# A hybrid decoder trunk on one core: the planner that spreads side work over the mixer's steps prices VectorE and TensorE operations anew

## The chip, the core and the metric

The kernel runs on one core of one Trainium2 chip, in one launch. The metric is device microseconds (us) of one execution; the time of a kernel is the median of several runs. A core has TensorE (PE in the rows; PEld is its weight loads), VectorE (DVE), ScalarE (ACT), GpSimd (POOL) and SyncE (SP), each with a queue of its own that it works through in order, and 16 DMA engines that all queues share.

## The reference, cut to what matters

One residual layer over 1024 tokens of width 1024. A mixer projects the normalised input once and runs three branches on it (stick-breaking attention, native sparse attention, a gated linear recurrence), gates and merges them and adds the result to the residual. Then a PEER layer chooses, for each token and each of 8 heads, 16 experts of 16384, and adds their output:

```python
h = rms_norm(x, norm_mix[l])
x = x + hybrid_mixer(h, ...)
h = rms_norm(x, norm_ffn[l])
x = x + peer_ffn(h, peer_w_q[l], peer_sub_keys[l], peer_u[l], peer_v[l])
...
s = jnp.einsum("nhad,akd->nhak", qh, sub_keys)
top_s, top_i = lax.top_k(s, K)
...
hpre = jnp.einsum("nd,nhkd->nhk", xc, u_tab[eidx])
act = gate * jax.nn.gelu(hpre)
return jnp.einsum("nhk,nhkd->nd", act, v_tab[eidx])
```

## The kernel before

The tokens are cut into four parts of 256 (parts 0 to 3). The mixer goes through the parts in order and through four heads or head groups in each. Its main work stands in a list of items, three to a head: the recurrence (`hg_items`), sparse attention (`nsa_items`) and stick-breaking attention (`sb_items`). An item has up to four stages, and the main loop (`while t < N + 3 or todo`) gives out, at step t, one stage each of items t, t-1, t-3 and t-2. There are 456 items. This text calls a head's stretch a round: round 2.3 is part 2, head 3, and begins where the recurrence's decay scan of that head (`b_hg`, L782) stands on VectorE.

All other work of the mixer is side work, cut into pieces (class `Piece`), each with an earliest and a latest step: the projections that feed a round (`pj_...`, each 24 matmuls of 256 columns at L265), the gates, and a part's tail: eight merges of the branches (`merge`, `pb` and `sg`), eight output projections (`wo`, `pj_wo`, with the residual's adds at L941), norms, the scores of the PEER router (`score_pieces`, `ts`) and the routing itself (`route`, tiles ending in `_rt`). For the middle parts 1 and 2, whose experts are computed densely, the routing is also spread into a matrix (`spread_pieces`): 64 blocks for each of these parts, 128 in all. A block is two operations on VectorE (L1219 and L1220, tile `hot`, 128x1024 in f16), eight small matmuls (L1223 and L1224, `gb`) and a copy on ScalarE; every fourth block writes 1 MB of the matrix `d_G` to memory.

Where a piece goes is decided by an estimate. `account()` adds to `load_["DVE"]` and `load_["PE"]` a price for each instruction given out. After each step the loop raises what is due: by `RDVE` (3.0) on VectorE, and on TensorE by 3.5, or by `PD` (1.2) times what VectorE got in this step where that is more, at most twice 3.5. As long as the load of an engine is below what is due, the next ready piece is given out: pieces marked `vector` (routing and spreading) on VectorE's account, all others on TensorE's:

```python
dv = load_["DVE"] - last_dve[0]
rate = min(max(rate, PD * dv), 2 * rate)
due[e] = min(max(due[e] + rate, load_[e] - 3 * rate), load_[e] + 2 * rate)
...
while load_[e] < due[e]:
    p = next((p for p in todo if ... p.ready(t + 1)), None)
```

A piece whose latest step comes is given out whatever the loads say. After the last item the loop goes on until no spread block is left; with each second of these blocks it gives out one piece of the tail of part 3 (list `ending`). What is left of `ending` goes, three pieces to an expert block, into the dense stage.

The dense stage follows: 128 expert blocks, each with 24 matmuls of 512 columns for the hidden values (`g`, L265), the factor from `d_G` (`gt`, L1434) and 24 matmuls for the output (`acc` and `g` at L1441). Parts 0 and 3 take their experts from memory by index: 1024 gathers of 128 rows (512 KB each), issued by GpSimd (L1149, L1159) and used by VectorE (L1151 `u`, L1161 `gacc`). Of these, 420 are tied to steps of the mixer (`paced()`: in proportion to `p + PB`, p being TensorE's estimated load of the step); the rest run beside the dense stage, and those of part 3 (512) need the routing of part 3.

In the end a scheduler of the language's library sets the order on each engine, from the order in which the program gives the work out.

## Time and profile before

| | |
|---|---|
| median of 3 runs | 3502.45 us (3502.05 to 3503.18) |
| the profiled execution | 3511.97 us, of which its span 3510.2 us |
| busy TensorE, VectorE, ScalarE, GpSimd | 3199.7, 3000.6, 1556.4, 1361.7 us |
| mean granted TensorE clock | 0.942 |
| bytes moved by DMA | 1058 MB, 301 GB/s over the span |

The profile's windows give, for a stretch of the span, each engine's busy time, the clock that TensorE was granted (1 is full speed) and the mean busy share of the 16 DMA engines. The chain of waits goes back from the end of a stretch to what released each step. The groups by line give busy time, mean ns of one instruction, and the idle time before them with what ended it. VectorE's busy time counts overlapping starts once, so it lies a little below the sum of its instructions' durations.

### The profile page before, as it was taken

The page shows a single profiled execution, that of the slowest core. Times are in us where ns is not written, and L with a number is a line of the kernel's source. Part 1 is how long each engine was busy: PE and PEld are TensorE (multiplying, and loading weights), DVE is VectorE, ACT ScalarE, POOL GpSimd, SP SyncE. Part 2 cuts the span into 40 slices and gives each one's busy share as a digit, 9 for nine tenths or more (in the row PEclk, how much of TensorE's full clock was granted, in tenths as well). Part 3 has the DMA queues.
Part 4 walks back from the last instruction along what each step waited for, and adds up shares of the span by engine and source line. Part 5 has one row for each costly group of instructions (what it writes and reads, how often), then busy time and mean ns, then how long its engine had stood idle before and what let it go on. Part 6 is the DMA issues. An engine that isn't in the chain of part 4 may idle for free.

```text
span 3510.2 us, 56907 instructions
## 1 busy us (share of the span) xinstructions
PE 3199.7 (91%) x20564; PEld 2175.3 (62%) x20564; DVE 3000.6 (85%) x6666; ACT 1556.4 (44%) x3181; POOL 1361.7 (39%) x1170
## 2 busy tenths in 40 slices
...
GB/s 305 334 248 147 308 185 226 320 314 310 358 284 231 199 289 291 327 332 259 191 250 154 344 372 312 241 271 387 392 384 329 385 367 362 362 368 375 367 358 219
DMA packets 359283, 1058.00 MB, mean 301 GB/s; under 512 B 35236, under 2 KB 107573, under 8 KB 354391
## 3 DMA queue, kind: packets, MB, share of 16 engines
...
q8 instruction: 161, 2.64, 0.3%
...
## 4 chain that ended last, share of the span: by engine, by line
PE 49%; DVE 23%; DMA 11%; issue 8%; ACT 6%; POOL 2%; SPq 0%; DVEq 0%; POOLq 0%; ACTq 0%
PE g L265 13%; PE acc L1441 10%; PE pj_mg L265 4%; DVE u L1151 3%; DVE gacc L1161 3%; PE g L1441 3%; DMA u<-in_peer_u_dram,gidx 3%; PE pj_r_hg L265 2%; DMA v<-in_peer_v_dram,gidx 1%; PE pb L265 1%; DMA gt<-d_G 1%; PE pj_wo L265 1%; POOL v L1159 1%; PE z_sb L417 1%; DMA vraw<-in_peer_v_dram 1%
## 5 line engine op out<-in xcount | busy, mean ns | idle before, releaser
L1159 POOL DMA_INDIRECT v<-in_peer_v_dram,gidx x421 | 556.0, 1321 | 674.0 <-DVE gacc L1161 348.4
L1149 POOL DMA_INDIRECT u<-in_peer_u_dram,gidx x417 | 529.7, 1270 | 596.6 <-DVE u L1151 367.4
L265 PE MATMUL g<-h,us 128*128 128x512 f16 x3072 | 688.2, 381 | 14.8 <-ACT ge L1400 12.1
L1441 PE MATMUL acc<-vs,ac 128*128 128x512 f16 x2304 | 542.2, 383 | 39.9 <-ACT vs L220 23.5
L1441 PEld LDWEIGHTS <-ac 128*128 128x128 f16 x3072 | 303.1, 99 | 426.1 <-issue 66.8
L1161 DVE SCALAR_TENSOR_TENSOR gacc<-v,act,gacc 128x1024 f32<-128x1024 f32 x421 | 538.9, 1280 | 29.4 <-DMA v<-in_peer_v_dram,gidx 25.8
L265 PEld LDWEIGHTS <-us 128*128 128x128 f16 x3072 | 301.6, 98 | 383.0 <-issue 21.1
L1151 DVE SCALAR_TENSOR_TENSOR u<-u,gh 128x1024 f32<-128x1024 f32 x417 | 501.9, 1219 | 33.2 <-DMA u<-in_peer_u_dram,gidx 32.7
L1400 ACT ACTIVATE ge<-g 128x512 f32<-128x512 f32 x128 | 76.1, 596 | 520.7 <-PE g L265 500.1
L265 PE MATMUL pj_mg<-hT,w_mg 128*128 128x256 f16 x2304 | 273.8, 275 | 4.0 <-ACT mg L885 4.0
L265 PEld LDWEIGHTS <-w_mg 128*128 128x128 f16 x2304 | 228.2, 100 | 33.6 <-issue 6.6
L1441 PE MATMUL g<-vs,ac 128*128 128x512 f16 x768 | 190.5, 388 | 11.6 <-ACT ge L1400 11.6
L1149 POOL DMA_INDIRECT rr_u<-in_peer_u_dram,gidx x95 | 134.2, 1413 | 96.7 <-DVE rr_u L1151 49.8
L221 DVE SCALAR_TENSOR_TENSOR vs<-vraw,vs 128x1024 f16<-128x1024 f32 x128 | 154.1, 1219 | 18.6 <-ACT vs L220 18.5
L221 DVE SCALAR_TENSOR_TENSOR us<-uraw,us 128x1024 f16<-128x1024 f32 x128 | 156.1, 1219 | 10.4 <-ACT us L220 10.3
L265 PE MATMUL pb<-o,w_b 128*128 128x256 f16 x1152 | 144.7, 281 | 21.1 <-DVE sg L923 15.1
L1159 POOL DMA_INDIRECT rr_v<-in_peer_v_dram,gidx x90 | 123.0, 1367 | 102.2 <-DVE gacc L1161 81.4
L220 ACT ACTIVATE vs<-vraw 128x1024 f16<-128x1024 f32 x128 | 131.0, 1046 | 55.0 <-DMA vraw<-in_peer_v_dram 55.0
L220 ACT ACTIVATE ac<-ge 128x512 f16<-128x512 f32 x128 | 79.9, 628 | 168.3 <-DVE ge L1434 139.0
L1434 DVE TENSOR_TENSOR ge<-ge,gt 128x256 f32<-128x256 f32 x256 | 98.4, 422 | 58.7 <-ACT ge L1400 44.9
L1223 PE MATMUL gb<-hot 128*128 128x128 f16 x512 | 125.7, 294 | 24.3 <-ACT stage L1226 13.1
L220 ACT ACTIVATE us<-uraw 128x1024 f16<-128x1024 f32 x128 | 134.2, 1048 | 21.4 <-PE g L265 12.8
...
## 6 DMA issues: line engine op xcount, KB each, us to landing
uraw<-in_peer_uT_dram SPq DMA_DIRECT2D x128, 512.0 KB, 7.7
vraw<-in_peer_v_dram SPq DMA_DIRECT2D x128, 512.0 KB, 7.2
...
gt<-d_G SPq DMA_DIRECT2D x32, 1024.0 KB, 17.5
...
```

Of the source, the lines that this page charges most:

```text
L220: S.activation(hi, src, AF.Copy, scale=scale)
L221: V.scalar_tensor_tensor(lo, in0=src, scalar=scale, in1=hi, op0=ALU.mult, op1=ALU.subtract)
L265: P.matmul(ps, l[:, k, :], r[:, k, :], start=(i == 0), stop=(i == n - 1))
L417: P.matmul(x["z"], qz[:, hh, tl * 128:(tl + 1) * 128], st["k"][:, r0 + c0:r0 + c1], start=True, stop=(c0 > 0))
L1149: G.indirect_dma_start(out=ur, out_offset=None, in_=a["peer_u"], in_offset=bass.IndirectOffsetOnAxis(ap=idx[:, c:c + 1], axis=0))
L1151: V.scalar_tensor_tensor(ur, in0=ur, scalar=1.0, in1=h2, op0=ALU.mult, op1=ALU.mult, accum_out=hpre[:, c:c + 1])
L1159: G.indirect_dma_start(out=vr, out_offset=None, in_=a["peer_v"], in_offset=bass.IndirectOffsetOnAxis(ap=idx[:, c:c + 1], axis=0))
L1161: V.scalar_tensor_tensor(acc, in0=vr, scalar=act[:, c:c + 1], in1=acc, op0=ALU.mult, op1=ALU.add)
L1223: P.matmul(ps[:, n, :], hs[:, 0, :, n], hs[:, 2, :, n], start=True, stop=False)
L1400: S.activation(ge, ps, AF.Gelu, scale=1.0 / (SW * SH2))
L1434: V.tensor_tensor(gv, gv, gt[:, :, i % 8, :], op=ALU.mult)
L1441: P.matmul(ps, ac[:, x, t * 128:(t + 1) * 128], v[:, y, dh * 512:(dh + 1) * 512], start=start and n == 0, stop=stop and n == 2)
```

## The change

Three prices and two rates are changed. An operation on VectorE cost 0.06 + n/960 us in the estimate, with n the elements of a partition; it costs 0.15 + n/960 now, with n halved where all operands have 16 bits, doubled for a scan, and 0.08 more for a search or replacement of maxima. A matmul on TensorE cost its columns at 2.4 GHz, four times that in 32 bits; it costs at least 0.11 now, and a transpose 0.11. `RDVE` goes from 3.0 to 3.45 and `PD` from 1.2 to 1.04. No operation is added, removed or altered.

```diff
--- before.py
+++ after.py
@@ -21,7 +21,7 @@
 
 
 
-RPE, RDVE, REND, PD = 3.5, 3.0, 5.0, 1.2
+RPE, RDVE, REND, PD = 3.5, 3.45, 5.0, 1.04
 
 PACE0, PACE, PB = 135, 420, 3.0
 
@@ -1099,10 +1099,16 @@
 
         ins = nc.cur_bb.bb.instructions
         for i in ins[seen[0]:]:
+            aps = [o for o in [*i.outs, *i.ins] if len(getattr(o, "ap", ())) > 1]
             if i.engine == mybir.EngineType.DVE:
-                load_["DVE"] += 0.06 + max([math.prod([x[1] for x in o.ap[1:]]) for o in [*i.outs, *i.ins] if len(getattr(o, "ap", ())) > 1] or [0]) / 960.0
+                n = max([math.prod([x[1] for x in o.ap[1:]]) for o in aps] or [0])
+                half = aps and all(mybir.dt.size(o.dtype) == 2 for o in aps)
+                twice = getattr(i, "is_tensor_tensor_scan", False)
+                more = 0.08 if isinstance(i, (mybir.InstMaxIndex, mybir.InstMatchReplace)) else 0.0
+                load_["DVE"] += 0.15 + more + n / 960.0 * (0.5 if half else 2.0 if twice else 1.0)
             elif i.engine == mybir.EngineType.PE:
-                load_["PE"] += math.prod([x[1] for x in i.outs[0].ap[1:]]) / 2400.0 * (4 if i.ins[0].dtype == F32 else 1)
+                n = math.prod([x[1] for x in i.outs[0].ap[1:]]) / 2400.0
+                load_["PE"] += 0.11 if i.is_transpose else max(0.11, n * (4 if i.ins[0].dtype == F32 else 1))
         seen[0] = len(ins)
 
     total_ = [0.0, 0.0]
```

What the new prices move can be read from the order of the two built programs. Up to round 2.0 (the first two parts) hardly anything moves. From there on, these counts differ (spread blocks, route operations and gathers by their place on VectorE, matmuls by their place on TensorE; "after items" begins with the first merge of part 3 and ends with the first dense block):

| round | spread blocks | route operations | gathers | `pj_wo` matmuls | `gb` matmuls |
|---|---|---|---|---|---|
| 2.0 | 0, 0 | 0, 0 | 44, 44 | 106, 168 | 0, 0 |
| 2.1 | 0, 0 | 1, 41 | 43, 45 | 86, 24 | 0, 0 |
| 2.2 | 1, 8.5 | 175, 135 | 32, 36 | 0, 0 | 0, 40 |
| 2.3 | 30, 47.5 | 0, 0 | 45, 42 | 0, 0 | 216, 376 |
| 3.0 | 16, 8 | 0, 0 | 34, 38 | 132, 48 | 144, 96 |
| 3.1 | 16, 0 | 1, 0 | 46, 42 | 60, 144 | 144, 0 |
| 3.2 | 5, 2 | 175, 170 | 34, 35 | 0, 0 | 8, 0 |
| 3.3 | 30, 46 | 0, 6 | 30, 30 | 0, 0 | 240, 352 |
| after items | 30, 16 | 0, 0 | 32, 31 | 120, 24 | 272, 160 |
| dense stage | 0, 0 | | | 72, 168 | 0, 0 |

In each pair the first number is of the kernel before, the second of the changed one. Other matmuls that move: in 2.2, 82 more of `pj_r_hg` and 24 more of `pj_i_hg`; in 2.3, 157 projection matmuls fewer (72 of them `pj_r_hg`); in 3.0, 61 projection matmuls more; in 3.2, 96 more of `pj_mg`, which 3.3 loses. The loop after the last item takes 22 steps where it took 36, and 60 pieces of `ending` are left for the dense stage where 53 were.

Three places on VectorE show it. The first is the start of round 2.3; `hot8` is the block of dense tokens 8 to 11, so the blocks stand in the order 0, 4, 8 and so on. Before:

```order
L1219 TENSOR_TENSOR hot0_14390<-iorep_139,spread1_14081 128x1024
L776 COPY_PREDICATED lf_hg3_2_14225<-tiny_hg3_2_14223,lf2_hg3_2_14228 128x256
L221 SCALAR_TENSOR_TENSOR hT3_14086<-tr_n3_0_0_14106,hT3_14086 128x4x128
L1220 TENSOR_TENSOR hot0_14390<-hot0_14390,spread1_14081 128x1024
L782 SCALAR_TENSOR_TENSOR b_hg3_2_14233<-lf_hg3_2_14225 128x128 x2
L791 TENSOR_TENSOR att_hg3_2_14305<-pd_hg3_2_14306,packed_106 128x256
L221 SCALAR_TENSOR_TENSOR hT3_14086<-tr_n3_0_1_14113,hT3_14086 128x4x128
L237 TENSOR_TENSOR u_n3_1_14131<-y_n3_1_14128 128x1
L238 TENSOR_TENSOR u_n3_1_14131<-u_n3_1_14131,ms_n3_1_14126 128x1
L239 TENSOR_SCALAR u_n3_1_14131<-u_n3_1_14131 128x1
L240 TENSOR_TENSOR y_n3_1_14128<-y_n3_1_14128,u_n3_1_14131 128x1
L291 SCALAR_TENSOR_TENSOR ht_n3_1_14122<-x_3_1_14120,y_n3_1_14128,gm3_14087 128x1024
```

And in the changed kernel (L1225 and L1226 are the same two lines, moved by six):

```order
L1225 TENSOR_TENSOR hot28_14519<-iorep_139,spread1_13990 128x1024
L1226 TENSOR_TENSOR hot20_14390<-hot20_14390,spread1_13990 128x1024
L776 COPY_PREDICATED lf_hg3_2_14320<-tiny_hg3_2_14318,lf2_hg3_2_14323 128x256
L1225 TENSOR_TENSOR hot32_14534<-iorep_139,spread1_13990 128x1024
L1226 TENSOR_TENSOR hot24_14403<-hot24_14403,spread1_13990 128x1024
L1167 SCALAR_TENSOR_TENSOR gacc_0_33005<-v0_72_33223,act_0_32617,gacc_0_33005 128x1024
L1226 TENSOR_TENSOR hot28_14519<-hot28_14519,spread1_13990 128x1024
L791 TENSOR_TENSOR att_hg3_2_14344<-pd_hg3_2_14345,packed_106 128x256
L782 SCALAR_TENSOR_TENSOR b_hg3_2_14328<-lf_hg3_2_14320 128x128 x2
L1225 TENSOR_TENSOR hot36_14585<-iorep_139,spread1_13990 128x1024
L1226 TENSOR_TENSOR hot32_14534<-hot32_14534,spread1_13990 128x1024
L1225 TENSOR_TENSOR hot40_14635<-iorep_139,spread1_13990 128x1024
```

The round began with block 0, beside the norm of the next part; it now begins nine blocks later, at `hot36`, and the norm has been done ahead of it.

The second place is in round 3.1, at the sparse attention of part 3 (`ns3g0t1`), beside the norm of part 2's PEER input (`f2`). Before:

```order
L580 TENSOR_TENSOR s_ns3g0t1_18079<-zc_ns3g0t1_18074,ct_ns3g0t1_18072 128x256
L238 TENSOR_TENSOR u_f2_1_17801<-u_f2_1_17801,ms_f2_1_17796 128x1
L582 TENSOR_REDUCE mx_ns3g0t1_18082<-s_ns3g0t1_18079 128x4
L239 TENSOR_SCALAR u_f2_1_17801<-u_f2_1_17801 128x1
L1219 TENSOR_TENSOR hot192_18031<-iorep_139,spread1_14081 128x1024
L583 TENSOR_TENSOR mx_ns3g0t1_18082<-mx_ns3g0t1_18082,nslope_128 128x4
L240 TENSOR_TENSOR y_f2_1_17798<-y_f2_1_17798,u_f2_1_17801 128x1
L1220 TENSOR_TENSOR hot192_18031<-hot192_18031,spread1_14081 128x1024
L291 SCALAR_TENSOR_TENSOR ht_f2_1_17792<-x2_2_1_17213,y_f2_1_17798,gf2_17749 128x1024
L591 RECIPROCAL zs_ns3g0t1_18085<-zs_ns3g0t1_18085 128x4
L1219 TENSOR_TENSOR hot196_18103<-iorep_139,spread1_14081 128x1024
L1219 TENSOR_TENSOR hot200_18150<-iorep_139,spread1_14081 128x1024
```

And now:

```order
L580 TENSOR_TENSOR s_ns3g0t1_18182<-zc_ns3g0t1_18177,ct_ns3g0t1_18175 128x256
L582 TENSOR_REDUCE mx_ns3g0t1_18185<-s_ns3g0t1_18182 128x4
L583 TENSOR_TENSOR mx_ns3g0t1_18185<-mx_ns3g0t1_18185,nslope_128 128x4
L591 RECIPROCAL zs_ns3g0t1_18188<-zs_ns3g0t1_18188 128x4
L594 TENSOR_TENSOR s_ns3g0t1_18182<-s_ns3g0t1_18182,zs_ns3g0t1_18188 128x256
L601 TENSOR_REDUCE imp_ns3g0t1_18259<-s_ns3g0t1_18182 128x16
L221 SCALAR_TENSOR_TENSOR h2_2_18030<-tr_f2_0_0_18031,h2_2_18030 128x4x128
L602 TENSOR_TENSOR imp_ns3g0t1_18259<-imp_ns3g0t1_18259,packed_106 128x16
L221 SCALAR_TENSOR_TENSOR h2_2_18030<-tr_f2_0_1_18038,h2_2_18030 128x4x128
L604 MAX m8_ns3g0t1_18262<-imp_ns3g0t1_18259 128x8
L232 TENSOR_SCALAR ms_f2_1_18050<-ss_f2_1_18047 128x1
L607 MATCH_REPLACE imp_ns3g0t1_18259<-m8_ns3g0t1_18262,imp_ns3g0t1_18259 128x16
```

The spread blocks that stood between the attention's operations are gone from here.

The third is the last stretch ahead of the dense stage, after the last stick-breaking item. Before:

```order
L1219 TENSOR_TENSOR hot480_22763<-iorep_139,spread2_20612 128x1024
L1220 TENSOR_TENSOR hot476_22719<-hot476_22719,spread2_20612 128x1024
L1219 TENSOR_TENSOR hot484_22776<-iorep_139,spread2_20612 128x1024
L941 TENSOR_TENSOR x2_3_22499<-x2_3_22499,tr_wo2_3_22789 128x128 x2
L1161 SCALAR_TENSOR_TENSOR gacc_1_33806<-v1_22_33874,act_1_33418,gacc_1_33806 128x1024
L1220 TENSOR_TENSOR hot480_22763<-hot480_22763,spread2_20612 128x1024
L1219 TENSOR_TENSOR hot488_22794<-iorep_139,spread2_20612 128x1024
L1220 TENSOR_TENSOR hot484_22776<-hot484_22776,spread2_20612 128x1024
L1219 TENSOR_TENSOR hot492_22807<-iorep_139,spread2_20612 128x1024
L1161 SCALAR_TENSOR_TENSOR gacc_1_33806<-v1_23_33877,act_1_33418,gacc_1_33806 128x1024
```

And now:

```order
L923 SCALAR_TENSOR_TENSOR sg6_3_22525<-pb0_6_3_22529,sg6_3_22525 128x256
L923 SCALAR_TENSOR_TENSOR sg6_3_22525<-pb1_6_3_22545,sg6_3_22525 128x256
L925 TENSOR_TENSOR sg6_3_22525<-sg6_3_22525 128x256
L1167 SCALAR_TENSOR_TENSOR gacc_1_33806<-v1_26_33886,act_1_33418,gacc_1_33806 128x1024
L923 SCALAR_TENSOR_TENSOR sg6_3_22525<-pb2_6_3_22562,sg6_3_22525 128x256
L925 TENSOR_TENSOR sg6_3_22525<-sg6_3_22525 128x256
L1225 TENSOR_TENSOR hot496_22720<-iorep_139,spread2_20612 128x1024
L1225 TENSOR_TENSOR hot500_22733<-iorep_139,spread2_20612 128x1024
L1226 TENSOR_TENSOR hot496_22720<-hot496_22720,spread2_20612 128x1024
L221 SCALAR_TENSOR_TENSOR m3_22040<-sg6_3_22525,m3_22040 128x256
L1167 SCALAR_TENSOR_TENSOR gacc_1_33806<-v1_27_33889,act_1_33418,gacc_1_33806 128x1024
L1226 TENSOR_TENSOR hot500_22733<-hot500_22733,spread2_20612 128x1024
```

Before, the merges (L923, L925) were done by here, and spread blocks, gathers and the residual's adds followed; now the merges last to the end, and fewer blocks stand between them. From the last `r_sb` subtraction (L432) to the first dense `us`, VectorE had 28 blocks, 31 gathers, 38 operations of merges and 6 adds; it has 14, 21, 38 and none.

## Rows read from the trace of the kernel before

**Rows 1.** Page: span; part 1, busy us (share of span) and instructions of each engine.

```profile
span 3510.2 us, 56907 instructions
...
PE 3199.7 (91%) x20564; PEld 2175.3 (62%) x20564; DVE 3000.6 (85%) x6666; ACT 1556.4 (44%) x3181; POOL 1361.7 (39%) x1170
```

**Rows 2.** One round's start, as the timeline prints it (start us, us, engine, line, operation).

```profile
1069.76 0.73 DVE L782 TENSOR_TENSOR_SCAN b_hg<-lf_hg 128x128 f32<-128x128 f32 x2
```

**Rows 3.** Windows, rounds 2.0 to 3.2: window, length, busy PE PEld DVE ACT POOL, PEclk, DMA, GB/s.

```profile
791.00:916.00 125.00, 116.18 (x952) 99.98 (x953) 103.50 (x252) 57.01 (x152) 49.70 (x51) 0.96 0.92 323
916.00:1070.00 154.00, 143.95 (x1187) 124.29 (x1187) 135.63 (x448) 70.59 (x184) 48.15 (x52) 0.99 0.83 304
1070.00:1192.00 122.00, 92.41 (x459) 71.66 (x457) 116.03 (x381) 57.86 (x149) 39.63 (x41) 0.64 0.61 202
1192.00:1353.00 161.00, 152.75 (x1282) 134.56 (x1282) 138.23 (x248) 81.71 (x202) 54.74 (x51) 0.96 0.79 279
1353.00:1490.00 137.00, 130.51 (x1046) 111.97 (x1045) 115.82 (x248) 71.08 (x166) 37.45 (x41) 0.98 0.88 315
1490.00:1662.00 172.00, 165.26 (x1354) 143.14 (x1354) 157.99 (x516) 87.06 (x200) 52.19 (x54) 1.00 0.85 297
1662.00:1796.00 134.00, 105.23 (x547) 75.97 (x546) 125.00 (x421) 64.00 (x149) 41.11 (x37) 0.73 0.58 191
```

**Rows 4.** Windows, same columns: round 3.3, the last items, the tail.

```profile
1796.00:1880.00 84.00, 72.08 (x511) 61.47 (x510) 79.99 (x168) 38.30 (x86) 25.74 (x24) 0.77 0.74 260
1880.00:1940.00 60.00, 46.02 (x268) 34.52 (x268) 39.42 (x69) 37.85 (x77) 15.98 (x14) 0.83 0.45 148
1940.00:2037.00 97.00, 75.31 (x620) 66.72 (x618) 83.47 (x133) 22.95 (x45) 33.43 (x27) 0.90 0.97 358
```

**Rows 5.** Windows, same columns: the dense experts' start, middle and late stretch.

```profile
2037.00:2140.00 103.00, 97.00 (x497) 49.16 (x498) 74.42 (x98) 44.32 (x61) 36.93 (x27) 0.97 0.99 349
2140.00:2375.00 235.00, 204.22 (x974) 99.67 (x973) 226.34 (x647) 70.39 (x94) 100.68 (x69) 0.93 0.82 272
2375.00:3487.00 1112.00, 1079.88 (x4957) 486.53 (x4955) 1023.77 (x1365) 366.30 (x485) 727.04 (x514) 0.99 0.98 364
```

**Rows 6.** Chain of waits by line, 2375 to 3487 us.

```profile
by line: PE g L265 36.8%; PE acc L1441 29.3%; issue 8.7%; PE g L1441 8.6%; DMA vraw<-in_peer_v_dram 3.4%; POOL v L1159 2.7%; DVE gacc L1161 2.1%; DMA gt<-d_G 1.7%; POOL rr_v L1159 1.6%; DVE vs L221 1.0%; DVE us L221 0.7%; DMA v<-in_peer_v_d
```

**Rows 7.** Groups by line, whole span: spread, gather, route and residual work on VectorE.

```profile
L1219 DVE TENSOR_TENSOR hot<-iorep,spread 128x1024 f16<-128x1024 f16 x128 | 86.8, 687 | 26.2 <-PE gb L1224 25.9
...
L1220 DVE TENSOR_TENSOR hot<-hot,spread 128x1024 f16<-128x1024 f16 x128 | 86.6, 685 | 0.3
...
L1161 DVE SCALAR_TENSOR_TENSOR gacc<-v,act,gacc 128x1024 f32<-128x1024 f32 x421 | 538.9, 1280 | 29.4 <-DMA v<-in_peer_v_dram,gidx 25.8
...
L1020 DVE FIND_INDEX8 ua_rt<-fa_rt,cand_rt 128x8 uint32<-128x72 f32 x64 | 13.6, 225 | 0.0
...
L941 DVE TENSOR_TENSOR x<-x,tr_wo 128x128 f32<-128x128 f32 x64 | 15.1, 281 | 8.8 <-PE tr_wo L282 8.7
```

**Rows 8.** Chain of waits, 1490 to 1662 us: start us, us, what.

```profile
1519.62 2.62 PE pj_r_hg L265 x24
```

**Rows 9.** Windows of tile hot alone: busy PE PEld DVE, PEclk, DMA, GB/s.

```profile
1192.00:1353.00 161.00, 29.13 (x216) 24.47 (x216) 40.59 (x61) 0.96 0.79 279
...
1490.00:1662.00 172.00, 19.86 (x144) 16.24 (x144) 21.71 (x32) 1.00 0.85 297
```

**Rows 10.** Groups by line, the tail (1940 to 2037 us).

```profile
L1161 DVE SCALAR_TENSOR_TENSOR gacc<-v,act,gacc 128x1024 f32<-128x1024 f32 x27 | 34.5, 1279 | 3.7 <-DMA v<-in_peer_v_dram,gidx 3.7
...
L1219 DVE TENSOR_TENSOR hot<-iorep,spread 128x1024 f16<-128x1024 f16 x28 | 19.1, 688 | 5.2 <-PE gb L1224 5.2
...
L265 PE MATMUL pj_wo<-m,w_wo 128*128 128x256 f16 x120 | 15.3, 284 | 0.0
```

**Rows 11.** Chain of waits, 2040 to 2120 us.

```profile
2036.73 12.27 DMA uraw<-in_peer_uT_dram
2052.70 20.25 DMA gt<-d_G
```

**Rows 12.** GpSimd's gather issues by line, round 2.1, then round 2.3.

```profile
L1159 POOL DMA_INDIRECT v<-in_peer_v_dram,gidx x39 | 44.2, 1134 | 90.3 <-DVE gacc L1161 32.3 <-DVE sv L984 17.3 <-DVE ts L988 7.4
...
L1159 POOL DMA_INDIRECT v<-in_peer_v_dram,gidx x45 | 55.2, 1227 | 102.9 <-DVE gacc L1161 86.4 <-DVE rz_ns2g1t1b2h L708 3.2 <-DVE r_sb L432 2.7
```

## The prediction

> **What bounds the kernel now.** I read the page first, for the span and the busy shares [rows 1]: TensorE 91% and VectorE 85%, so neither is the bound everywhere, and shares alone decide nothing. Then the windows, cut at the rounds; a round begins where the decay scan stands in the timeline, as round 2.2 at 1069.76 us [rows 2]. The reader is to see two kinds of rounds in the mixer [rows 3]. In 2.0, 2.1, 2.3, 3.0 and 3.1 TensorE is busy for 93% to 96% at nearly the full clock, and VectorE for 83% to 92%: TensorE sets the length. In 2.2 and 3.2, where the routing of parts 1 and 2 runs, it is the reverse: VectorE is busy for 95% and 93%, TensorE for 76% and 79%, at a mean granted clock of 0.64 and 0.73. Work that goes from the first kind to the second on TensorE, and the other way on VectorE, should cost less where it arrives than where it leaves.
>
> The end of the mixer has three stretches [rows 4]: round 3.3, bound by VectorE (80 of 84 us); 60 us of the last items, in which no engine is over 77%; and a tail of 97 us, in which the merges of part 3 run beside 28 spread blocks, with VectorE at 86%, TensorE at 78% and DMA at 0.97. The dense stage [rows 5] starts with TensorE busy for 97 of 103 us, then has 235 us bound by VectorE (226 busy; the routing of part 3 is here), and a late stretch of 1112 us with TensorE at 97%. There the chain of waits is TensorE's matmuls for three quarters (36.8% + 29.3% + 8.6%) [rows 6]. So a matmul that is put into the dense stage counts, unless it fits into the gaps of the first 338 us (6 + 31 us).
>
> **The change part by part.** No operation is added or removed; every term is a move. Prices: a spread block is 0.687 + 0.685 us on VectorE, a gather's addition 1.28, a route operation 0.22, an add of the residual 0.28 [rows 7]; 24 matmuls of 256 columns take 2.62 us on the chain, 0.109 each [rows 8]; the small `gb` matmuls take 29.13/216 = 0.135 each in round 2.3 and 19.86/144 = 0.138 in 3.1 [rows 9]. The counts are those of the table and the text on the change.
>
> Up to round 2.0 nothing: the orders are all but the same.
>
> Round 2.0: 62 more `pj_wo`, 6.8 us, and six transposes. TensorE bounds the round: +7. Ends: 0 (in the 9 us of its idle time) and +7.
>
> Round 2.1: 72 matmuls fewer, -8 on TensorE. But VectorE gets 40 route operations (8.8) and two gathers (2.6), less six adds (1.7), and would be busy for 145 of 154 us, near its 95% in round 2.2. I take half the gain, -4; ends -8 and +2.
>
> Round 2.2: VectorE, the bound, gets 7.5 blocks (10.3), four gathers (5.1) and a norm's row and splits (3.3) for 40 route operations less (8.8): +10. TensorE gets 146 matmuls more, some 17 us, and would be busy for 109 us of 132: hidden, as long as VectorE leaves it gaps. Ends +5 and +13.
>
> Round 2.3: TensorE gets 160 `gb` (21.6) and loses 157 projection matmuls (17.1) and some transposes: +3.6. VectorE gets 17.5 blocks (24.0), less three gathers and the norm's part (7.8): +16, so 154 of 161 us, 96%. That just fits: +3. If none of VectorE's 23 us of idle time can be used, +16; the other end is 0.
>
> Round 3.0: TensorE loses 84 `pj_wo` (9.2) and 48 `gb` (6.5), gets 61 others (6.6), and loses eight transposes: -10. VectorE loses 8.5 too, so it does not stand in the way. Round 3.1: -144 `gb` (19.9), +84 `pj_wo` (9.2), -19 others: -12, with VectorE 25 us lighter. Were VectorE's waits part of what holds TensorE here, the round could lose up to those 25; the other end is -6 for each of the two.
>
> Round 3.2: VectorE loses three blocks and some route operations, gets one gather: -4. Its 115 more matmuls on TensorE lie beside VectorE, as in 2.2. Ends -6 and 0.
>
> Round 3.3 and the last items (144 us, VectorE busy for 119): 16 blocks (22.0), nine gathers that have left the tail (11.5) and six route operations come in: +35 on VectorE. All of it on the path would be +35; filled to 100%, 154 us, it would be +11. Filled to the 95% of round 2.2, it is 162 us, +19; the last items wait for one another, so I take +24.
>
> Tail: it loses ten gathers, 14 blocks and six adds: 12.8 + 19.2 + 1.7 = 34 us of VectorE's 83 [rows 10], and 112 `gb` and 96 `pj_wo` on TensorE, 26 us of 75. At VectorE's share of 86% that is -39, at TensorE's 78% -33; by DMA, ten gathers (512 KB each), 3.5 MB of `d_G` and four weights of 512 KB, 11 MB at 358 GB/s, -30. I take -34; ends -39 and -21 (the 14 blocks' own 19.2 and the adds alone). On SP's queue the weights of the moved `wo` steps now come behind the first `uraw` loads. The waits that open the dense stage, 12.3 us for `uraw` and 20.3 for `gt` [rows 11], stay: the last block still ends just ahead of it.
>
> Dense stage: 96 `pj_wo` and six transposes more, 10.5 us. TensorE is the bound in most of it: +10; ends 0 (in the gaps of 6 and 31 us) and +13.
>
> Sum: 7 - 4 + 10 + 3 - 10 - 12 - 4 + 24 - 34 + 10 = **-10 us**. Against the profiled execution of 3511.97 us that is 3502; the median of the runs is 9.5 us lower, 3502.45, and the same sum gives 3492 there. I call 0.2%, 7 us, the least that a measurement of this kernel can tell from no change.
>
> One cost I hold at zero, GpSimd's issues in round 2.3, where 95 `hot` operations stand now for 60. The rows show no hold: a gather's issue took 1.227 us there with 61 `hot` operations beside it, and 1.134 in round 2.1 without any [rows 12], 0.09 us that GpSimd's idle 106 us cover. The Trainium skill, "SBUF — State Buffer", section "Who interferes with whom", speaks against the change here: an operation of VectorE with two SBUF inputs, as `hot` has, holds a shared read port for its whole length against a GpSimd instruction that reads SBUF (that the making of a DMA's descriptors is such a read, the same section does not claim; it infers the opposite). By that rule each added `hot` could hold an issue for 0.69 us, and the sum would be +14 instead of -10; the trace disagrees so far, by the 0.09 us above.
>
> **The rivals.**
>
> *Slower: VectorE fills up where the blocks arrive.* Rounds 2.3 and 3.3 get 16 and 35 us of VectorE's work and stand at 86% and 83% now. If the chains inside the items, not the sum, use the idle time, these rounds grow by all of it (+13 and +11 over my terms), the tail gives 4 less, 2.1 gives nothing (+4), and the total is -10 + 32 = +22: 3524. It decides from the point at which round 2.3 is longer than 170 us. For it: in 2.2 and 3.2 VectorE never passes 95% even as the sole bound. Against it: 3.1 held TensorE at 96% and VectorE at 92% at once. Chance 0.25.
>
> *Even: the tail's gain is eaten by its neighbour.* Round 3.3 and the last items take the full +35 while all else is as forecast: +1 in all, 3503. Chance 0.18.
>
> *Faster by more.* Round 3.1 follows VectorE (-25, 13 more), the tail and its neighbour give -39 and +11 (18 more), the dense stage hides its matmuls (10 more): -51, 3451. It needs all three; chance 0.10.
>
> *Slower: GpSimd's issues are held.* In 2.3, 35 added `hot` operations by 0.686 us are 24 us in which no gather is issued; if VectorE, which works in order, waits for each of these, the total is +14, 3516. VectorE's additions waited for a gather's data for only 29.4 us in the whole span [rows 7]; chance 0.03. The hold is the one that the page of the Trainium skill named above states.
>
> That the change does not move the work is excluded by the built order, which shows it.
>
> **How the numbers follow.** The forecast keeps 0.44. Its own range, from single terms at their ends, is some 3480 to 3505. The range of 8 in 10 leaves out the half of the large gain and the far end of the slower case: 3462 to 3528. Faster by over 0.2% (under 3495.4): most of the forecast, 0.37, and the large gain, 0.10. Slower (over 3509.5): 0.25 + 0.03, and 0.03 from the others. Within: the remaining 0.22.
>
> **What would show it.** Right: rounds 3.0 and 3.1 shorter by some 10 us each, 2.2 longer by 10, the tail from the last stick-breaking item to the first dense matmul near 63 us, and the dense stage longer by some 10, with `pj_wo` in its first stretch. Wrong: round 2.3 over 170 us, a tail that stays over 80 us (then DMA or the merges' own chain bound it, not the blocks), or a late dense stretch whose TensorE share falls below 97%, which would say that the later routing of part 3 pushes its gathers into each other.

## The result and the profile after

The changed kernel is slower: 3536.43 us (3528.97 to 3537.99, 4 runs) against 3502.81 us for the kernel before on the same chip (3502.05 to 3503.99, 4 runs), a ratio of 1.0091 with an interval of 1.0074 to 1.0109. The forecast was 3492 us, faster; the result has the other sign and lies outside the range of 3462 to 3528. The profiled execution of the changed kernel took 3537.99 us, 1.6 over its median; that of the kernel before lay 9.2 over its own. So the profiles differ by 26 us where the medians differ by 34, and 8 us of the loss can't be put to a place. All times here and below are medians of undisturbed runs: two slow ones, of e2 (5541 us) and of the kernel before beside e9 to e12 (4143 us), are left out.

The page of the changed kernel, which answers to [rows 1]:

```profile
span 3536.2 us, 56972 instructions
PE 3196.2 (90%) x20564; PEld 2166.5 (61%) x20564; DVE 2999.9 (85%) x6666; ACT 1561.1 (44%) x3186; POOL 1369.9 (39%) x1170
```

The shares are those of before, within 1%. The windows say more. Rounds 2.0 to 3.2, then round 3.3, the last items and the tail, columns as in [rows 3, 4]:

```profile
787.00:910.00 123.00, 116.65 (x988) 101.78 (x987) 104.96 (x258) 62.53 (x158) 48.36 (x51) 0.99 0.95 345
910.00:1068.00 158.00, 141.98 (x1107) 119.79 (x1106) 141.89 (x502) 74.92 (x185) 52.17 (x54) 0.94 0.82 288
1068.00:1200.00 132.00, 105.19 (x669) 86.09 (x668) 127.09 (x349) 65.18 (x168) 45.15 (x44) 0.76 0.66 223
1200.00:1362.00 162.00, 150.36 (x1233) 132.53 (x1231) 150.01 (x269) 87.13 (x204) 59.55 (x49) 0.95 0.84 288
1362.00:1488.00 126.00, 120.38 (x976) 103.02 (x975) 110.13 (x238) 69.84 (x164) 45.43 (x45) 0.99 0.93 337
1488.00:1651.00 163.00, 154.80 (x1256) 130.44 (x1256) 136.06 (x473) 74.12 (x181) 49.22 (x50) 1.00 0.81 288
1651.00:1792.00 141.00, 116.70 (x660) 86.71 (x659) 122.00 (x416) 68.82 (x151) 44.94 (x37) 0.75 0.56 189
1792.00:1909.00 117.00, 92.44 (x599) 75.85 (x597) 111.26 (x232) 57.30 (x124) 36.06 (x31) 0.68 0.68 240
1909.00:1947.00 38.00, 27.78 (x193) 21.40 (x191) 32.61 (x42) 26.06 (x53) 14.65 (x11) 0.99 0.54 164
1947.00:2028.00 81.00, 56.85 (x435) 47.99 (x435) 60.45 (x98) 16.90 (x33) 25.48 (x21) 0.86 0.90 336
```

Against [rows 3, 4] round 2.2 is 10 us longer, 3.0 and 3.1 are 11 and 9 shorter, 3.2 is 7 longer, round 3.3 with the last items 11 longer, the tail 16 shorter. The mixer ends at 2028 us, some 10 earlier, where 20 were forecast. The loss is behind it. From here on the dense stage is cut from its first `g` matmul to its last matmul into `acc`, and in two where VectorE uses the first gathered row of part 3. The changed kernel:

```profile
2028.00:2387.00 359.00, 314.41 (x1579) 160.36 (x1579) 303.75 (x757) 120.45 (x165) 129.51 (x101) 0.93 0.83 284
2387.00:3522.00 1135.00, 1091.86 (x4989) 490.04 (x4988) 1021.96 (x1365) 364.10 (x484) 720.27 (x508) 0.98 0.96 355
```

The kernel before, cut in the same way (cut by round numbers, it is [rows 5]):

```profile
2038.00:2386.00 348.00, 312.23 (x1520) 153.82 (x1521) 309.21 (x760) 122.19 (x165) 143.78 (x101) 0.95 0.87 296
2386.00:3496.00 1110.00, 1077.88 (x4948) 485.58 (x4945) 1019.12 (x1357) 362.64 (x482) 720.97 (x509) 0.99 0.97 361
```

The dense stage is 1494 us in place of 1458, 36 longer. TensorE's busy time grew by 16 us (96 `pj_wo` matmuls and six transposes more; at 0.109 each some 11), and its idle time by 20: from 36 to 45 us in the early part, from 32 to 43 in the late one. The other 5 us of busy time go with a lower granted clock (0.93 and 0.98 for 0.95 and 0.99). So some 25 us of the 36 are no work that the change put there.

Most of the early 9 us lies ahead of the first `acc` matmul: up to it, TensorE is idle for 4 us in the kernel before and for 11 in the changed one. The last wait there, before and after:

```profile
2074.18 7.94 PE L1441 MATMUL acc<-vs,ac 128*128 128x512 f16 x36 [2.34 <-ACT ac L220]
2064.31 6.38 PE L1447 MATMUL acc<-vs,ac 128*128 128x512 f16 x18 [10.72 <-ACT ac L220]
```

This matmul needs the first factors (`gt`), whose load takes 20.25 us before [rows 11] and 21.22 now, and in both kernels it starts 36 us after the first `g` matmul. What differs is the work that TensorE has in the meantime: 120 `g` matmuls before and 96 now, 6 us less of busy time. The `g` matmuls of one expert block now come behind the wait instead of filling it.

Where the late idle time lies, the timeline shows. TensorE's largest late stall, and two typical ones:

```profile
2822.28 1.01 PE L1447 MATMUL acc<-vs,ac 128*128 128x512 f16 x2 [4.74 <-ACT vs L220]
2919.33 1.01 PE L1447 MATMUL acc<-vs,ac 128*128 128x512 f16 x2 [8.64 <-ACT vs L220]
3361.86 1.01 PE L1447 MATMUL acc<-vs,ac 128*128 128x512 f16 x2 [5.45 <-ACT vs L220]
```

They come in steps of some 90 us, which is eight dense blocks. Of the six that are longer than 2 us, five stand before a matmul that needs a freshly loaded block of V (`vraw`, split into `vs`); the sixth, 6.30 us at 3015 us, waits for a copy on ScalarE that stands behind the split of such a block. Each eight blocks the factors change (`gt`, two halves of 1 MB in three buffers). SyncE's queue around the largest (columns: start, length with its wait, line, what):

```profile
2870.78 2.70 SPq L100 DMA_DIRECT2D vraw<-in_peer_v_dram  x2
2882.37 4.21 SPq L1435 DMA_DIRECT2D gt<-d_G  x2
2886.63 16.26 SPq L100 DMA_DIRECT2D uraw<-in_peer_uT_dram  x1
2902.99 1.25 SPq L100 DMA_DIRECT2D vraw<-in_peer_v_dram  x1
```

The load of V at 2902.99 us, the last of the old eight blocks, stands behind both factor loads, which need buffers that VectorE has still to use up, and behind a load of U that held the queue for 16.26 us. The queue's own waits from 2860 to 2912 us (columns: us in all, times, longest) put 16.2 us to that load (L100) and 9.1 to the factor loads (L1435), both until VectorE has done a product with the factors (`ge`):

```profile
SPq L100 <- DVE ge L1440: 18.3, 2, 16.2
SPq L1435 <- DVE ge L1440: 9.1, 1, 9.1
```

So this largest stall is not the factor loads' alone. The chain of waits goes on from there: the load is issued at 2902.99 us and takes 15.21 among the gathers, where the median load of V takes 7.0:

```profile
2902.99 15.21 DMA vraw<-in_peer_v_dram
2918.22 1.06 ACT vs L220
2919.33 1.01 PE acc L1447 x2
```

In the kernel before, at the change from block 63 to block 64, the same queue runs otherwise: the last two loads of V of the old eight blocks (the first row) stand ahead of the factors, and TensorE did not wait there, although a load of U held the queue here too.

```profile
2769.63 1.46 SPq L100 DMA_DIRECT2D vraw<-in_peer_v_dram  x2
2773.61 6.83 SPq L1429 DMA_DIRECT2D gt<-d_G  x2
2780.50 13.05 SPq L100 DMA_DIRECT2D uraw<-in_peer_uT_dram  x2
2793.66 1.74 SPq L100 DMA_DIRECT2D vraw<-in_peer_v_dram  x2
```

One change later, in the same kernel, the last two (blocks 70 and 71, the last row) stand behind the factors, and TensorE waited for them, 3.4 us in all:

```profile
2841.24 1.46 SPq L100 DMA_DIRECT2D vraw<-in_peer_v_dram  x2
2856.35 8.24 SPq L1429 DMA_DIRECT2D gt<-d_G  x2
2864.65 5.56 SPq L100 DMA_DIRECT2D uraw<-in_peer_uT_dram  x2
2870.31 0.85 SPq L100 DMA_DIRECT2D vraw<-in_peer_v_dram  x2
```

Of the 15 changes, the queue has a load of V of the old eight blocks behind the factors at five in the kernel before (both loads there) and at eight in the changed one (one load). The late stalls around changes (at the last two old blocks and the first new one) sum to 26.9 us before, 22 of them at the five, and to 36.6 after, 30 at the eight. The sums differ by 9.7 us, nearly all of the late difference; whether the order at the changes makes it is for the experiments.

### The profile page after: what moved, and what is told of

The parts are those of the page before. It is cut to its first block, busy times and chain, and to the rows that moved or that the text cites. A ratio compares the mean times of both kernels' runs of the same rounds, so it can differ in the third digit from the quotient of the medians.

```text
span 3536.2 us, 56972 instructions
## 1 busy us (share of the span) xinstructions
PE 3196.2 (90%) x20564; PEld 2166.5 (61%) x20564; DVE 2999.9 (85%) x6666; ACT 1561.1 (44%) x3186; POOL 1369.9 (39%) x1170
## 4 chain that ended last, share of the span: by engine, by line
PE 47%; DVE 24%; DMA 11%; issue 9%; ACT 7%; POOL 2%; SPq 0%; DVEq 0%; POOLq 0%; ACTq 0%
PE g L265 13%; PE acc L1447 10%; DVE gacc L1167 4%; PE pj_mg L265 4%; DVE u L1157 3%; PE g L1447 2%; DMA vraw<-in_peer_v_dram 2%; DMA u<-in_peer_u_dram,gidx 2%; PE pj_r_hg L265 2%; DMA gt<-d_G 2%; PE pj_wo L265 1%; PE pb L265 1%; DMA v<-in_peer_v_dram,gidx 1%; POOL u L1155 1%; DVE ts L986 1%
## 5 line engine op out<-in xcount | busy, mean ns | idle before, releaser
L265 PE MATMUL g<-h,us 128*128 128x512 f16 x3072 | 697.3, 384 | 25.8 <-ACT ge L1406 12.1
L1155 POOL DMA_INDIRECT rr_u<-in_peer_u_dram,gidx x95 | 142.5, 1500 | 57.9 <-DVE rr_u L1157 32.2
L265 PE MATMUL pj_r_hg<-hT,w_r_hg 128*128 128x256 f16 x1152 | 139.9, 279 | 7.0 <-ACT v_sb L399 3.6
```

The costliest lines, as they stand in the source:

```text
L265: P.matmul(ps, l[:, k, :], r[:, k, :], start=(i == 0), stop=(i == n - 1))
L1155: G.indirect_dma_start(out=ur, out_offset=None, in_=a["peer_u"], in_offset=bass.IndirectOffsetOnAxis(ap=idx[:, c:c + 1], axis=0))
```

## The experiments

All runs in one table. The mixer's end and the dense stage (first `g` to last `acc`), and TensorE's idle time in its early and late part, are read from the trace of each run; the times are medians, the ratio is to the kernel before on the same chip.

| run | us | ratio | mixer end | dense stage | idle early, late |
|---|---|---|---|---|---|
| before (first job) | 3502.81 | | 2038 | 1458 | 36, 32 |
| the change | 3536.43 | 1.0091 [1.0074, 1.0109] | 2028 | 1494 | 45, 43 |
| e1 | 3596.51 | 1.0274 [1.0235, 1.0313] | 2068 | 1509 | 51, 46 |
| e2 | 3570.09 | 1.0179 [1.0115, 1.0243] | 2060 | 1495 | 40, 59 |
| e3 | 3529.54 | 1.0088 [1.0058, 1.0118] | 2052 | 1457 | 36, 39 |
| e4 | 3533.03 | 1.0090 [1.0060, 1.0121] | 2036 | 1467 | 47, 17 |
| e5 | 3553.43 | 1.0148 [1.0128, 1.0168] | 2043 | 1486 | 53, 36 |
| e6 | 3526.43 | 1.0072 [1.0044, 1.0099] | 2023 | 1476 | 45, 22 |
| e7 | 3503.48 | 0.9997 [0.9982, 1.0012] | 2036 | 1426 | 21, 23 |
| e8 | 3530.74 | 1.0085 [1.0060, 1.0109] | 2023 | 1484 | 57, 29 |
| e9 | 3553.75 | 1.0136 [1.0118, 1.0154] | 2036 | 1503 | 41, 56 |
| e10 | 3574.31 | 1.0185 [1.0153, 1.0216] | 2026 | 1528 | 45, 68 |
| e11 | 3494.49 | 0.9963 [0.9949, 0.9978] | 2038 | 1444 | 35, 22 |
| e12 | 3518.20 | 1.0043 [1.0028, 1.0057] | 2024 | 1478 | 44, 31 |
| e13 | 3501.76 | 0.9993 [0.9979, 1.0007] | 2023 | 1472 | 50, 21 |
| e14 | 3508.67 | 1.0009 [0.9990, 1.0027] | 2025 | 1462 | 42, 20 |
| e15 | 3513.04 | 1.0022 [1.0004, 1.0040] | 2041 | 1452 | 48, 18 |
| e16 | 3511.48 | 1.0031 [1.0016, 1.0046] | 2016 | 1473 | 45, 20 |
| e17 | 3511.61 | 1.0022 [1.0008, 1.0036] | 2023 | 1464 | 48, 19 |
| e18 | 3507.86 | 1.0010 [0.9995, 1.0024] | 2021 | 1462 | 39, 17 |

**e1 and e2: one half of the change each.** e1 is the changed kernel, its new rates kept, with the old price of a matmul:

```diff
-                n = math.prod([x[1] for x in i.outs[0].ap[1:]]) / 2400.0
-                load_["PE"] += 0.11 if i.is_transpose else max(0.11, n * (4 if i.ins[0].dtype == F32 else 1))
+                load_["PE"] += math.prod([x[1] for x in i.outs[0].ap[1:]]) / 2400.0 * (4 if i.ins[0].dtype == F32 else 1)
```

> The changed kernel with the old prices on TensorE (VectorE's new prices, RDVE 3.45 and PD 1.04 kept). It leaves 22 spread blocks after the last item and gives out 9 tail pieces there, as the changed kernel does. Theory A (the dense stage pays for the seven tail pieces of part 3 that the shorter loop leaves to it): 3525 to 3540 us, with the dense stage, first dense matmul to last, over 1480 us. Theory B (the loss is an accident of how the dense stage's loads and the gathers meet in the new order): any time from 3490 to 3540, no relation to the 9 pieces. If TensorE's prices were the cause: 3495 to 3505.

e2 is the kernel before with the new price of a matmul, the same lines the other way round.

> The kernel before with TensorE's new prices alone (VectorE's old prices, RDVE 3.0, PD 1.2). 35 blocks and 16 tail pieces after the last item, as before. Theory A: 3495 to 3510 us. Theory B: the dense stage may differ from that of before by up to 30 us although the same 52 pieces are left to it.

Both times lie above every range of their expectations. Each half alone is slower than both together: the mixer ends 40 us (e1) and 32 us (e2) later than with both, and the dense stage is 15 us longer in e1 and as long in e2. The dense stage of e2 has the very matmuls and transposes of the kernel before, and is still 37 us longer than there, outside theory B's 30 too. So the pieces left are not needed for the loss.

**e3 and e4: the pieces alone.** e3 is the changed kernel, which gives out a tail piece with each spread block; e4 the kernel before, which stops at 60 pieces left.

```diff
-EVERY = 2
+EVERY = 1
```

> The changed kernel with EVERY = 1: a tail piece of part 3 with each spread block of the last loop, so 20 instead of 9 go ahead of the dense stage. Theory A: the mixer ends some 10 to 15 us later than in the changed kernel (11 pieces, some 130 matmuls), the dense stage is 35 to 45 us shorter; in all 3495 to 3515 us. Theory B: 3515 to 3545 us, or anything without a link to the number of pieces.

```diff
-                if left % EVERY == 0 and ending and left > EVERY and left != seen_left[0]:
+                if left % EVERY == 0 and len(ending) > 60 and left > EVERY and left != seen_left[0]:
```

> The kernel before, with the tail pieces in the last loop ended at 8 instead of 16 (the merges alone), so that 8 more are left to the dense stage; all else of the planner as before. Theory A: the mixer ends 10 to 15 us earlier and the dense stage is 30 to 45 us longer; 3518 to 3535 us. Theory B: 3490 to 3515 us, the dense stage longer by no more than the 10 to 12 us of the moved matmuls.

e3 gets the dense stage back to 1457 us, but pays 24 us in the mixer. e4's dense stage grows by 9 us, less than the 13 that its 120 moved `pj_wo` matmuls take, with less late idle time than before. Its total of 3533 us is in theory A's range, but not by A's mechanism: VectorE uses the last gathered row 17 us behind the last matmul. Theory A is half right at best.

**e5 and e6: prices that change at round 3.3.** The old and the new lines of `account()` and the rates stand side by side, chosen by the step (e6 the other way round):

```diff
+    t_now[0], CUT[0] = 0, start[3, 3, "hg"]
...
+        was = t_now[0] >= CUT[0]
+        rdve, pd = (3.0, 1.2) if was else (RDVE, PD)
```

> The changed kernel, whose planner goes back to the old prices and rates from the step at which round 3.3 begins. The order of rounds 2.0 to 3.2 is nearly that of the change, the end (round 3.3, the last items, the tail with 32 spread blocks, 53 pieces left for the dense stage) that of the kernel before. Theory A (the dense stage pays for the later routing of part 3, which the shorter tail leaves to it): the dense stage, first dense matmul to last matmul into acc, is 1458 us as before, within 8; rounds 2.0 to 3.2 as in the changed kernel (+2 us against before, the earlier rounds -5), the tail as before; in all 3493 to 3507 us. Theory B (an accident of how loads and gathers of the dense stage meet in the order that the scheduler makes): the dense stage is 1475 us or more and the total over 3515.

> The mirror of it: the old prices and rates up to round 3.3, the new ones from there. The mixer is that of the kernel before up to 3.2; then 48 blocks in round 3.3, 12 in the tail, 192 pj_wo matmuls in the dense stage (72 before, 168 in the changed kernel). Theory A: the dense stage is 1490 to 1510 us (13 us of matmuls and the later routing), round 3.3 to the first dense matmul 0 to 10 us shorter than the 242 before; in all 3530 to 3550 us. Theory B: the dense stage is longer by its 13 us of matmuls at most, 1458 to 1472; in all 3500 to 3515.

e5 has the end of the kernel before, 53 pieces left, and still a dense stage of 1486 us; e6 has the end of the changed kernel, 192 `pj_wo` matmuls in the dense stage, and one of 1476, 18 us longer than before with 19 us more of busy time. e5 is as theory B had it, e6 lies between the two theories. The dense stage depends on the order that comes before it at least as much as on what is left for it.

**e7 and e8: the routing of part 3 later and earlier, the mixer untouched.**

```diff
-TP, LEAD = 3, 3
+TP, LEAD = 2, 3
```

> The kernel before with two pieces of part 3's tail to a dense block in place of three: the mixer's order is untouched, the 53 pieces take 27 blocks in place of 18, so the routing of part 3 ends some 80 to 90 us later, at about 445 us of the dense stage in place of 360. No work is added. Theory A: the dense stage grows, by 30 us or more (in the changed kernel, 15 us later cost some 25 beyond the added matmuls); in all 3535 us or more. Theory B: no matter when the gathers of part 3 begin, they fit beside TensorE: the dense stage stays within 15 us of 1458, the total between 3490 and 3520.

e8 sets 4 in the changed kernel.

> The changed kernel with four pieces of part 3's tail to a dense block in place of three: the mixer's order is untouched, the 60 pieces take 15 blocks in place of 20, so the routing ends some 40 to 50 us earlier than in the changed kernel, at about 330 us of the dense stage. Theory A: the dense stage gives back most of its loss, 1450 to 1468 us, and the total is 3493 to 3512. Theory B: the dense stage stays at 1480 us or more, the total within 12 us of the changed kernel's 3536.

e8 did not do what it was to do: the first route operation of part 3 came 32 us earlier than in the changed kernel, but the last one 23 us later (399 us into the dense stage for 376). The dense stage is 1484 us and the total 3531, as theory B had it, but nothing follows from that for an earlier routing.

e7 refutes the theory that the later routing costs TensorE. The last route operation comes 68 us later (428 us into the dense stage for 360), and the dense stage is 32 us *shorter*, more than theory B's 15; the gathers end behind it, so that the total is that of before. Its late part, and what is left behind the last matmul:

```profile
2398.00:3462.00 1064.00, 1041.03 (x4793) 469.71 (x4790) 982.21 (x1326) 342.41 (x454) 716.09 (x498) 0.99 0.98 366
3462.00:3506.00 44.00, 0.00 (x0) 0.00 (x0) 38.02 (x58) 8.68 (x22) 14.78 (x13) 0.54 0.64 227
```

TensorE and DMA are both busy for 97 to 98% here: two loads that fill the same 1100 us. Which of them ends last differs from run to run: the gathers in e4, e6 and e7, TensorE in both kernels.

Over these ten traces the stall of TensorE around a change of the factors goes with the order on SP's queue: 5.1 us on average where both loads of V of the old blocks stand behind the factors (29 changes), 3.0 us where one does (24), 0.7 where the last stands just ahead (38). Of the other 59, with loads of V for the new blocks ahead as well, 38 lie in the late part (1.0 us on average) and 21 in the early one (9.8 us, where other waits fall on the same blocks). That became theory D.

**e9 and e10: the order forced, one way and the other.** e9 puts, in the kernel before, both loads of V behind both factor loads at every change (the factors are traced two blocks early, and `gload` is the last of them):

```diff
+        for q in sorted({i // 8, min(i + 2, NI - 1) // 8}):
...
+                    gload = next(x for x in reversed(nc.cur_bb.bb.instructions) if x.engine == mybir.EngineType.SP)
+        with tc.issue_after(gload):
+            raw = load(late.tile([128, D], F32, tag="vraw", name=f"vraw{i}", bufs=2), a["peer_v"][i * 128:(i + 1) * 128, :])
```

> The kernel before, with one order forced on SP's queue in the dense stage: at each of the 15 changes to the next eight dense blocks, the loads of V for the last two blocks of the old eight (vraw) stand behind both loads of the new factors (gt), which wait until VectorE has used the old factors up. Theory D (what the change moved and the prediction did not look at is this place on SP's queue): in the ten traces so far TensorE stood still for 5.1 us on average around a change where both loads of V stand behind (29 changes), 3.0 us where one does (24), 0.7 us where the last load of V stands just ahead of the factors (38). Before has five changes of the first kind; with 15 of them the dense stage grows by 35 to 60 us, the total is 3535 to 3565. Theory E (the late dense stretch is bound by DMA, which is busy for 97% there and moves some 400 MB in every trace; the stalls are where the waiting shows, not what makes it): the order does not matter, the total stays within 12 us of 3504.

The dense stage grew by 45 us, the total by 48: as theory D had it. No byte and no operation was added. The late part:

```profile
2400.00:3539.00 1139.00, 1083.45 (x4933) 485.64 (x4931) 1020.24 (x1354) 366.34 (x485) 716.55 (x505) 0.98 0.95 352
```

Against the kernel before, TensorE's idle time over the whole dense stage is 29 us longer, and its busy time 16 us for the same work, at a granted clock of 0.94 and 0.98 in the two parts for 0.95 and 0.99. e10 puts, in the changed kernel, the factors behind V of the first block that needs them:

```diff
-                nc.sync.dma_start(gt, d_G[c:c + 16, :, i // 8 * 8:i // 8 * 8 + 8, :].rearrange("c p i n -> p c i n"))
+                with tc.issue_after(vload):
+                    nc.sync.dma_start(gt, d_G[c:c + 16, :, i // 8 * 8:i // 8 * 8 + 8, :].rearrange("c p i n -> p c i n"))
```

> The changed kernel with the other order forced: the factors are loaded behind V of the first block that needs them (vraw of block 8m), at every change. In the changed kernel eight of the 15 changes have a load of V behind the factors. Theory D: eight stalls of 3 to 4 us go, 24 to 32 us, and the total is 3502 to 3516, unless the factors, issued later now, are themselves late. Theory E: the total stays at 3525 to 3545.

A miss, by the clause that its expectation ends with: now the factors were late. VectorE's waits for them in the late part (columns: us in all, times, longest), 12.1 us in 3 waits in the changed kernel:

```profile
DVE ge L1442 <- DMA gt<-d_G: 77.4, 15, 9.2
```

So neither order is good while a change needs two buffers and one is free.

**e11 and e12: no wait for a buffer in the queue.** The halves change four blocks apart, each loaded two blocks ahead into the buffer that is free.

```diff
-        if i // 8 not in gts:
+        for n in range(k, min(k + 3, NI)):
+            for c in (0, 16):
+                q = (n + c // 4) // 8
+                if (c, q) not in gts:
+                    lo, hi = max(q * 8 - c // 4, 0), min(q * 8 - c // 4 + 8, NI)
...
+                    with tc.issue_after(vload):
+                        nc.sync.dma_start(gt[:, :, :hi - lo, :], d_G[c:c + 16, :, lo:hi, :].rearrange("c p i n -> p c i n"))
```

> The kernel before, with the two halves of the factors changed four blocks apart (one at blocks 8m, the other at 8m+4), so that of the three buffers one is always free for the next half, which is loaded behind V of the block two ahead of its first use: no load waits for a buffer in the queue and none is late. The same bytes, the same operations. Theory D: TensorE's idle time in the late stretch, 32 us, falls to 10 or less, and the total to 3478 to 3492, where the last gathers (23 us ahead of the last matmul now) stop it. Theory E: no change, 3495 to 3512.

> The changed kernel with the same staggered factors. Theory D: the 43 us of idle time of TensorE in the late stretch fall to 10 or less, the total to 3492 to 3508, so that what is left between this kernel and e11 is 10 to 20 us: the matmuls added to the dense stage and the idle time that opens it, less what the mixer gained. Theory E: the total stays at 3520 to 3540, 25 or more above e11.

e11 and e12, late parts:

```profile
2378.00:3481.00 1103.00, 1081.42 (x4975) 488.16 (x4974) 1020.94 (x1356) 360.40 (x480) 719.72 (x509) 0.99 0.98 364
```

```profile
2381.00:3502.00 1121.00, 1090.24 (x5006) 491.16 (x5004) 1028.15 (x1374) 364.54 (x486) 695.56 (x508) 0.99 0.96 359
```

e11 is the version that beats both kernels: 0.37% below the kernel before (interval 0.22% to 0.51%). In neither does a factor load wait in SyncE's queue in the late part any more. But both results miss theory D's ranges by 2.5 and 10 us, and lie only 0.5 and 1.8 us below those of theory E: late idle time fell by 10 and 12 us, to 22 and 31, not to 10. And since both kernels gained nearly the same, the dense stages still differ by 34 us for 36, and the late idle times by 9 for 11. So the order at the changes costs both kernels time, but it is not what sets the two apart.

**e13 to e16: what is left between them.** e13 is e12 with seven tail pieces given out ahead of the first dense block:

```diff
+    for p in ending[:7]:
+        p.emit(1 << 20)
+    del ending[:7]
     for k, i in enumerate(order):
```

> e12 with the first seven pieces of part 3's tail given out ahead of the first dense block, so that 53 are left for the blocks as in the kernel before. The dense stage of the changed kernel opens with a stall of 10.7 us (8.2 in e12), in which TensorE waits for the first factors and the weights of the tail pieces stand behind them on SP's queue. Theory F (the pieces that the shorter tail left are the cause: they come late, one block after the other, and leave this gap open): the gap is filled, the dense stage falls from 1478 to 1460 to 1468 us, the total from 3518 to 3500 to 3510. Theory G (the places of part 3's gathers among the dense blocks on VectorE are the cause) and theory H (nothing in particular, many small waits): 3512 to 3524.

e14 is e12 with part 3's gathers held on VectorE behind dense blocks:

```diff
+        if ti // 2 == PARTS[-1].i:
+            third[0] += 1
+            return tc.issue_after(used[min(int(26 + third[0] / 5.12), NI - 1)])
```

> e12 with part 3's gathers held back on VectorE: the r-th may stand no earlier than behind the factor of dense block 26 + r/5.12. The order has the 128th, 256th and 384th of them at blocks 51, 78 and 104 then, as in e11 (51, 78, 103); in e12 they stand at 50, 76 and 102. Theory G: the dense stage falls to 1450 to 1462 us (e11's 1444 and the added matmuls), the total to 3492 to 3505. Theories F and H: the total stays at 3510 to 3524, or rises, since gathers that are held back end later.

e15 is e5 with the staggered factors, e16 is e6 with them.

> e5 (new prices up to round 3.3, old ones after; 53 pieces left) with the staggered factors. e5's dense stage was 1486 us with the 53 pieces of the kernel before, 28 us more than there. Theory D (the order on SP's queue at the changes): most of its excess goes, the dense stage is 1450 to 1460 us, the total 3518 to 3528. Theory H: it gains as e11 and e12 did, 11 to 18 us, and the total is 3534 to 3544.

> e6 (old prices up to round 3.3, new ones after; 64 pieces left; the mixer ended at 2023 us, 15 earlier than in the kernel before) with the staggered factors. By the gain of e11 and e12, 11 to 18 us: 3508 to 3516. Theory F (pieces left) has it slower than e11 in the dense stage by 20 us or more; if the pieces cost their matmuls alone (192 pj_wo for 72, 13 us), the total is 3490 to 3500 and the kernel no slower than e11.

e14: the late idle time fell from 31 us to 20 (e11: 22), and the dense stage from 1478 to 1462, in theory G's range at its end; the total, 3508.67, fell by 9.5 and not by the 13 or more that it asked for. Over e11 18 us are left in the dense stage: 13 of busy time, by the added matmuls and transposes, and 7 of early idle time, less 2 of late. So the late difference between the two kernels went with e14's edit (e13 and e14 ran on another chip than e12). But it went in e13 too, whose late idle time is 21 us, and there part 3's gathers begin 18 us earlier in the dense stage than in e12, while in e14 they begin 10 us later. What makes the late difference is not shown by this. e13's total fell by 16, as theory F said, but not in the way it said: the gap at the start is still there,

```profile
2058.30 2.31 PE L1454 MATMUL acc<-vs,ac 128*128 128x512 f16 x5 [10.66 <-ACT ac L220]
```

and the dense stage of its trace is only 6 us shorter; that execution was 9 us over the median, so the rest of the gain can't be placed. e15 gained 40 us on e5 and 34 in the dense stage: there the changes were the excess, more clearly than theory D asked. e16 gained 15 and lies where the gain of e11 and e12 puts it; its dense stage stays 29 us above e11's, as theory F had it: 20 us of busy time (120 `pj_wo` and 36 `pb` matmuls and six transposes more) and 9 of idle time. That the pieces left make the idle time is not shown, since round 3.3 has another order too.

**e17 and e18: all of it together.** e12 and e16 with the additions of e13 and e14 (e18 gives out eleven pieces) and with the first factors queued ahead of U of the fourth block:

```diff
+        with tc.issue_after(first[0]) if i >= 3 else ExitStack():
+            load(raw, a["peer_uT"][i])
```

> The changed kernel with everything that helped: the staggered factors (e12), part 3's gathers held to their places (e14), the first seven tail pieces ahead of the first dense block (e13), and the first factors loaded ahead of U of the fourth block (uraw) on SP's queue, which is meant to close the gap at the start of the dense stage. If the three gains stand beside each other, the dense stage is 1450 to 1462 us (e11's 1444 and 10.5 us of added matmuls), the mixer ends at 2023 to 2027, 11 to 15 us ahead of the kernel before, and the total is 3482 to 3496, no slower than e11 (3494). If they take from each other (each only moves where the gathers and the loads meet), it stays at 3500 to 3510.

> The same additions to e16 (old prices up to round 3.3, new ones after; eleven pieces given out ahead of the first dense block). Its mixer ended at 2016 to 2023 us. If the gains stand beside each other, the dense stage is 1452 to 1465 us and the total 3480 to 3495; if not, 3500 to 3512 (e16: 3511).

Neither reached its first range, and e17 lies 2 us over its second one too: the gains take from each other. In e17 the late part is as good as in e11 (1095 us for 1103, idle 19 for 22), the mixer ends 15 us earlier, and the early part is longer than all that, 369 us:

```profile
2023.00:2392.00 369.00, 321.32 (x1613) 163.21 (x1612) 310.01 (x772) 122.81 (x168) 156.57 (x105) 0.94 0.84 292
```

against 340 in e11, with 121 more rows on TensorE and 13 us more of idle time. What the added pieces cost there beyond their matmuls was not taken apart; it stays open.

## Why the prediction was wrong

- **Round 2.2, +10; 2.3, +3; 3.0, -10; 3.1, -12.** Measured +10, +1, -11, -9. These came from counts and rows of a round whose bound was known, and held.
- **Round 2.0, +7, and 2.1, -4.** Measured -2 and +4, both 2 us outside their ends. In 2.0 TensorE's busy time stayed at 116 us with 36 rows more, at a granted clock of 0.99 for 0.96. In 2.1 it fell by only 2 us with 80 rows less, at 0.94 for 0.99, and VectorE went from 136 to 142 us. The sum took the clock of both rounds as it was.
- **Round 3.2, -4.** Measured +7, outside its ends. VectorE's busy time fell from 125 to 122 us as counted, but it waited 10.2 us for ScalarE inside the stick-breaking item, 1.1 before.
- **Round 3.3 and the last items, +24; tail, -34.** Measured +11 (155 us for 144) and -16 (81 for 97): their sum, -5 for -10, was better than the terms, and that is luck. The tail did not come to 63 us; at 81 it stayed over the line of 80, over which the prediction had DMA or the merges' own chain as the bound, and one load of weights for the merges (`w_b`) alone is 16.26 us of the chain there.
- **The dense stage, +10 (0 to +13): this step failed.** Its 96 matmuls and six transposes cost what was said, some 11 us. But the step took TensorE's idle time in the stage to stay as it was, and looked only for gaps to hide matmuls in. Measured +36: beside the matmuls 20 of idle time (9 early, 11 late) and 5 of lower clock. Early, the prediction rightly said that the waits that open the stage stay, but not that TensorE would have less to do in them: 7 of the 9 us are there. Of the late 11 us, in a stretch where TensorE and DMA are both at 96 to 97%, 9.7 lie at the changes of the factors. That the order on SP's queue makes time there is shown by e9 (+45 us with nothing added), and e15 shows most of an excess of that kind go. It does not explain the two kernels, though: with it taken out of both (e11, e12), 9 us of late idle time are still between them. These went in e13 and in e14, with part 3's gathers begun earlier in the one and later in the other: what makes the late difference stays open.
- **The sign of being wrong was named, its cause was not.** TensorE's share of the late stretch fell below 97% (1091.86 of 1135 us, 96.2%), as the last of the prediction's signs had it. The cause given there, that the later routing of part 3 pushes its gathers into each other, fell with e7: a routing that ended 68 us later came with a dense stage 32 us shorter.
- **The rivals.** The slower rival's time, 3524, was nearer than the forecast's, but its mechanism did not occur: round 2.3 took 162 us, not over 170, so that its nearness is luck. Nor did those of the even and the faster rival: round 3.3 with the last items took 11 us more and not 35, and the dense stage did not hide its matmuls. GpSimd's issues were not held at the price that the rule would give. In round 2.3 they took 1.399 us on average with 95 `hot` operations, for 1.227 with 61 [rows 12]: 0.17 us times 43 issues is 7 us, in 103 us of idle time.

```profile
L1165 POOL DMA_INDIRECT v<-in_peer_v_dram,gidx x43 | 60.1, 1399 | 103.1 <-DVE gacc L1167 77.8 <-DVE nmx_ns2g1t1b1h L675 9.3 <-DVE att_hg L827 4.9
```

The rule is that of the Trainium skill, "SBUF — State Buffer", section "Who interferes with whom"; a rise there is, but far from the 24 us that a hold for each added operation would be.
